# Low parts on GpSimd and a fourth seven-product unit in gate and up of a transformer block

## Chip, cores and metric

The kernel runs on one core of a Trainium2 chip. The metric is the device time of one execution in microseconds (us); before the change it is 1452.65 us (median of 3 runs, 1452.64 to 1453.78). Engines: TensorE (PE; PEld are its weight loads), VectorE (DVE), ScalarE (ACT), GpSimd (POOL) and SyncE (SP), which issues most of the transfers.

## What is computed

One block of an encoder on a sequence of 256 positions and width 2048: four mixers and an output product, cross attention with 256 memory positions, and a gated feed-forward layer with 5632 hidden units, everything in float32. The part that matters here is the last:

```python
D_FF = ((8 * D_MODEL // 3 + 255) // 256) * 256     # 5632

def swiglu(h, w_gate_up, w_down):
    gate, up = jnp.split(h @ w_gate_up, 2, axis=-1)
    return (jax.nn.silu(gate) * up) @ w_down
...
        x = x + swiglu(rms_norm(x, norm_g[l, 2]), w_gate_up[l], w_down[l])
    return rms_norm(x, final_norm_g)
```

## The kernel before, in words

**Splitting.** Products run at float32 accuracy on TensorE by splitting each operand into a high part, rounded to the type that TensorE multiplies (`F32R`), and a low part, the rest. One product of a 128 x 128 block of activations with 128 x 512 weights is then three matmuls: high by high, high by low, low by high (`Block.part`, lines 493 to 498). The weights come from memory as plain float32. `Stream.split` (line 150) makes the parts: ScalarE copies `raw` to `wh` with rounding (L156), and VectorE subtracts `wl = raw - wh` (L157).

**Stream.** All weights are laid out on the host in the order of their use, in slabs of 128 x 2048 (1 MB, one transfer by SyncE's queue, L136). `Stream.make` splits a slab in parts of 1024 columns, each into one buffer pair `wh`, `wl`; in gate and up there are five such pairs, and four slots for raw slabs. A part is made as soon as a pair is free, up to a bound, so some parts are ready ahead of TensorE.

**Gate and up.** `gate_up` goes over 11 columns `j` of 512 hidden units. For each it multiplies by 512 columns of gate and 512 of up, over 16 blocks of the inner dimension, taken in 8 pairs `i`. A plain pair is one slab: 2 inner blocks x 2 (gate, up) x 2 halves of the rows, 8 products of three matmuls, 24 in all. Its slab is two parts of 1024, hence two casts and two subtractions.

**Seven-product units.** For the pairs named by `sevens(j)` the 2 x 2 x 2 products are formed with seven products instead of eight, by sums of blocks (Winograd's form of Strassen's scheme): 21 matmuls. The sums of activation blocks are made once, ahead, by `left` (they stay in SBUF as `sh` and `sl`); the sums of weight blocks are made on VectorE in place in the raw slab (L189), and the slab is split in four parts of 512, 1024, 1024 and 1024. Before the change the units are pairs 1, 3 and 5 in every column, except the first, which has only 5. Four of the seven products go to banks of their own (`p1`, `p5`, `p7`, `p6`), which `combine` adds on VectorE after the last unit of the column (the copy of `p1` on ScalarE is L1000); three go to the banks of the plain pairs. `finish` then adds the two kinds of banks, applies silu and the product, transposes the hidden block on VectorE (`store_turned`, L525) and has GpSimd issue eight transfers to the `hidden` tensor in memory (L530). `finish` of one column runs during the first pairs of the next one.

**Other work of GpSimd's queue there.** `turn` writes the residual to `xrows`, transposed (L1077), and reads it back (L1081); `fetch` reads the stored hidden blocks for the down product (L941). All of these are transfers that wait for VectorE or for earlier transfers, and an engine's queue is served in order.

**Order.** Matmuls are in the order of the program. Side work is held in generators (`Background`), which are polled between products and step on by an estimate of time. The order of each engine's instructions is then settled by the framework when the program is built; `keep` ties the parts of a unit to their places, plain parts are not tied.

Of the kernel before, what the change touches and what calls it, by code (L numbers as in the profile page):

```python
# [13 lines left out]
F32 = mybir.dt.float32  # L14
# [4 lines left out]
ALU = mybir.AluOpType  # L19
# [31 lines left out]
GU = 16 * (40 + 16 + 16 + 32 + 16)  # L51

def sevens(j):

    return (1, 3, 5) if j else (5,)


FORMED = 6
# [20 lines left out]
DOWN = GU // 16 + 16 * DFF // 1024  # L79
# [6 lines left out]
def seven(slab):  # L86

    j, i = divmod(slab - GU // 16, 8)
    return slab in UNITS if slab >= DOWN else j >= 0 and i in sevens(j)
# [22 lines left out]
class Stream:  # L112
# [34 lines left out]
                return pool  # L147
        return None

    def split(self, pool, at, r, edges):  # L150

        nc = self.nc
        wh, wl = (pool.tile([P, 1088], F32R, name=t, tag=t) for t in ("wh", "wl"))
        wh, wl = wh[:, at:at + 1024], wl[:, at:at + 1024]
        for a, b in zip(edges, edges[1:]):
            nc.scalar.copy(wh[:, a:b], r[:, a:b])  # L156
            nc.vector.tensor_tensor(out=wl[:, a:b], in0=r[:, a:b], in1=wh[:, a:b].bitcast(F32), op=ALU.subtract)  # L157
        self.bg.dve(edges[-1], len(edges) - 1)
        self.items.append((pool, wh, wl))

    def make(self):

        nc, (slab, part) = self.nc, self.todo
        n = 16 * slab + 8 * part
        if n >= NBLK - HELD:
            parts = [(self.places.pop(0)) for _ in range(2)]
            r = self.raw(slab)[:, part * 1024:part * 1024 + 1024]
            for a, (wh, wl) in zip((0, 512), parts):
                nc.scalar.copy(wh, r[:, a:a + 512])
                nc.vector.tensor_tensor(out=wl, in0=r[:, a:a + 512], in1=wh.bitcast(F32), op=ALU.subtract)  # L170
            self.bg.dve(1024, 2)
            self.items.append((None, parts))
            self.todo = (slab + part, 1 - part)
            return True
        pool = self.free(slab)
        if pool is None:
            return False
        raw = self.raw(slab)
        at = 48 if any(a <= n < b for a, b in ROWS) else 8
        r = raw[:, part % 2 * 1024:part % 2 * 1024 + 1024]  # L180
        if not seven(slab):
            mark = len(nc.cur_bb.bb.instructions)
            self.split(pool, at, r, [0, 256, 512, 1024] if n == 0 else [0, 512, 1024] if n == 8 else [0, 1024])
            if DOWN <= slab < DOWN + 2 * AHEAD:
                self.keep(mark)
            self.todo = (slab + part, 1 - part)
            return True
        mark = len(nc.cur_bb.bb.instructions)
        op = lambda out, a, b, what=ALU.subtract: nc.vector.tensor_tensor(out=out, in0=a, in1=b, op=what)  # L189
        self.split(pool, at, r, [0, 512] if part == 0 else [0, 1024])  # L190
        b11, b12, b22, b21 = (raw[:, a:a + 512] for a in range(0, 2048, 512))
        if part == 0:
            blk = raw.rearrange("p (b c) -> p b c", b=4)
            op(r.rearrange("p (b c) -> p b c", b=2), blk[:, 0:3:2, :], blk[:, 1:2, :].to_broadcast([P, 2, 512]))
            self.bg.dve(1024)
        elif part == 1:
            op(b22, b22, b11, ALU.add)
            op(b21, b21, b22)
            self.bg.dve(1024, 2)
        self.keep(mark)  # L200
        self.todo = (slab + part // 3, (part + 1) % 4)
        return True
# [87 lines left out]
class Block:  # L290
# [665 lines left out]
    def gate_up(self, sw, gp, f):  # L956

        nc, st = self.nc, self.st
# [6 lines left out]

        def left():

            for i in (5, 1, 3):
                t = [self.tmp() for _ in range(2)]
                for x, k in zip(t, (2 * i, 2 * i + 1)):  # L970
                    nc.scalar.activation(x, self.resk(k), AF.Copy, scale=self.gvec(V_NG + 32, k))
                (a11, a21), (a12, a22) = ((x[:, 0:P], x[:, P:R]) for x in t)
                s = gp.tile([P, 512], F32, name="u", tag="u", bufs=2)
                s1, s2, s3, s4 = (s[:, a:a + P] for a in range(0, 512, P))
                self.stt(s1, a21, -1.0, a22, ALU.mult, ALU.subtract)
                self.stt(s2, s1, -1.0, a11, ALU.mult, ALU.subtract)
                self.tt(s3, a11, a21, ALU.subtract)
                self.tt(s4, a12, s2, ALU.subtract)
                yield
                h, l = sums[i] = [sw.tile([P, 512], F32R, name=f"s{x}{i}") for x in "hl"]  # L980
                self.split2(h, l, s)
                yield
# [44 lines left out]

        ready = [self.late, self.bg.add(norm())]
        forms = self.bg.add(left())
        turned = self.bg.add(self.turn())  # L1030
        early = end = None
        for j in range(DFF // 512):
# [5 lines left out]
            for i in range(8):  # L1038
                if j >= NUDGE and i in (2, 4, 7):
                    self.bg.nudge(turned if i == 2 else early)  # L1040
                if j == 0 and i == 6:
                    for g in ready:
                        self.bg.drain(g)
                if i == 1 and end:
                    self.bg.drain(end)
                if i in sevens(j):
                    if i == sevens(j)[0]:
                        if j == 0:
                            self.bg.drain(forms)
                        ps = [banks[1 - j % 2]() for _ in range(4)]  # L1050
                    unit(i, cs, ps, i == sevens(j)[0], i == sevens(j)[-1], *cols)
                    if i == sevens(j)[-1]:
                        s = [[gp.tile([P, 512], F32, name=f"{n}{r}", tag=f"{n}{r}") for n in "gh"] for r in range(2)]
                        last = combine(ps, s)
                        self.bg.add(last)
                    continue
                for k in (2 * i, 2 * i + 1):
                    for c in range(2):
                        wh, wl = st.take("w_gate_up", k, cols[c], 4)
                        for r in range(2):  # L1060
                            self.part_rows(cs[r][c], r, self.h3[k], wh, wl, k == 0, k == KT - 1)
                            self.bg.poll()
# [816 lines left out]
```

## Time and profile before

| | |
|---|---|
| median of 3 runs | 1452.65 us |
| the profiled execution | 1454.31 us, of it 1452.4 us from the first to the last instruction (its span) |
| mean granted TensorE clock | 0.998 |
| gate and up, from the first column's `combine` to the last one's (ten columns' time) | 414.8 us |

The page of the profile gives busy time by engine, the chain that ended last, and the costliest groups of instructions. A group's row has the line, the engine, the operation, what it writes and reads, the count, then busy time and mean duration in ns, then idle time in front of it and who ended it. A row of the timeline has its start, its length, engine and line, and in brackets the idle time before it; equal instructions that follow each other share a row (`x8`), and where shapes are mixed the row shows the first. A row of the stretches of time has the bounds, the busy time of each engine with the number of instructions, the granted clock, the share of transfers and their rate.

### The profile page before, as it was taken

What the parts mean: (1) busy time and instruction counts of PE and PEld (TensorE: products, weight loads), DVE (VectorE), ACT (ScalarE), POOL (GpSimd) and SP (SyncE); (2) the same over time, 40 slices, a digit from 0 to 9 for tenths busy, and PEclk for the clock granted to TensorE, in tenths of its full rate; (3) what the DMA queues carried; (4) which work ended last, traced back from release to release, by engine and by line L of the source; (5) the groups of instructions that cost most, each with busy time, mean ns of one, the idle gap of its engine ahead of it and who ended that gap; (6) DMA issues with size and microseconds to landing.
All of it is one profiled execution on the core that took longest, in us unless ns stands there. A gap on an engine that the chain in (4) does not pass through costs nothing.

```text
span 1452.4 us, 19765 instructions
## 1 busy us (share of the span) xinstructions
PE 1439.1 (99%) x7231; PEld 1217.8 (84%) x7231; DVE 1192.3 (82%) x1750; ACT 844.1 (58%) x1254; POOL 172.2 (12%) x294
## 2 busy tenths in 40 slices
PE   9999999999999999999999999999999999999997
PEld 8888888898899888888888888888888888788886
DVE  6587768778868767877778999999999997988875
ACT  6565655466656646765565555555655564655554
POOL 0220100000000001100003334112111112100000
PEclk9999999999999999999999999999999999999999
DMA  9985654454535656555555767666667656655654
GB/s 352 339 289 197 220 193 168 152 187 156 195 129 206 215 179 224 172 170 195 178 205 205 277 234 243 220 209 237 233 220 250 221 200 220 214 184 199 225 203 146
DMA packets 57394, 307.17 MB, mean 211 GB/s; under 512 B 9773, under 2 KB 11470, under 8 KB 25680
## 3 DMA queue, kind: packets, MB, share of 16 engines
q1 hardware_dynamic: 45920, 281.11, 54.9%
q0 software_dynamic: 10944, 24.14, 5.4%
q8 instruction: 57, 0.93, 0.3%
q10 hardware_dynamic: 432, 0.66, 0.1%
q14 instruction: 41, 0.34, 0.1%
HBM read 291.71 MB, written 14.16 MB: 211 GB/s over the span
## 4 chain that ended last, share of the span: by engine, by line
PE 94%; DVE 2%; issue 2%; ACT 1%; DMA 1%; POOL 1%; SPq 0%; DVEq 0%; POOLq 0%; ACTq 0%
PE pg L444 19%; PE pg L496 13%; PE pg L497 13%; PE pg L495 13%; PE pg L445 10%; PE pm L496 6%; PE pm L495 6%; PE pm L497 6%; PE pm L1380 1%; DVE wl L157 1%; PE pg L441 1%; PE pg L442 1%; PE pm L895 1%; PE pm L868 1%; DMA tmp<-hidden 1%
## 5 line engine op out<-in xcount | busy, mean ns | idle before, releaser
L156 ACT CAST wh<-raw 128x1024 fp32r<-128x1024 f32 (+1 forms) x589 | 589.2, 1013 | 466.6 <-PE pg L497 149.7
L157 DVE TENSOR_TENSOR wl<-raw,wh 128x1024 fp32r<-128x1024 f32 (+1 forms) x589 | 681.4, 1175 | 177.8 <-ACT wh L156 171.7
L444 PE MATMUL pg<-act,wh 128*128 128x512 f32 x1104 | 387.5, 393 | 0.0
L445 PE MATMUL pg<-act,wl 128*128 128x256 f32 x1216 | 340.7, 280 | 0.0
L496 PE MATMUL pg<-wl,act 128*128 128x512 f32 (+1 forms) x689 | 268.3, 389 | 1.5 <-DVE wl L157 1.4
L495 PE MATMUL pg<-wh,act 128*128 128x512 f32 (+1 forms) x689 | 268.7, 391 | 0.0
L497 PE MATMUL pg<-wh,act 128*128 128x512 f32 (+1 forms) x689 | 268.3, 389 | 0.0
L444 PEld LDWEIGHTS pg<-act,wh 128*128 128x128 f32 x1104 | 207.4, 188 | 44.9
L445 PEld LDWEIGHTS pg<-act,wl 128*128 128x128 f32 x1216 | 228.5, 188 | 0.8 <-DVE wl L157 0.5
L496 PEld LDWEIGHTS pg<-wl,act 128*128 128x128 f32 x689 | 129.5, 188 | 29.6 <-DVE wl L157 3.1
L495 PEld LDWEIGHTS pg<-wh,act 128*128 128x128 f32 x689 | 129.6, 188 | 27.5 <-issue 0.8
L497 PEld LDWEIGHTS pg<-wh,act 128*128 128x128 f32 x689 | 129.4, 188 | 27.4 <-issue 0.4
L496 PE MATMUL pm<-wl,act 128*128 128x512 f32 x318 | 123.7, 389 | 0.0
L497 PE MATMUL pm<-wh,act 128*128 128x512 f32 x318 | 123.7, 389 | 0.0
L495 PE MATMUL pm<-wh,act 128*128 128x512 f32 x318 | 123.6, 389 | 0.0
L189 DVE TENSOR_TENSOR raw<-raw 128x1024 f32<-128x1024 f32 x129 | 111.7, 866 | 3.0
L530 POOL DMA_DIRECT2D hidden<-u x88 | 56.8, 653 | 162.3 <-DVE u L525 139.7
L495 PEld LDWEIGHTS pm<-wh,act 128*128 128x128 f32 x318 | 59.7, 188 | 12.5
L497 PEld LDWEIGHTS pm<-wh,act 128*128 128x128 f32 x318 | 59.7, 188 | 12.4
L496 PEld LDWEIGHTS pm<-wl,act 128*128 128x128 f32 x318 | 59.7, 188 | 12.4
L1077 POOL DMA_DIRECT2D xrows<-tmp x64 | 37.0, 586 | 182.7 <-DVE rc L323 126.6
L941 POOL DMA_DIRECT2D tmp<-hidden x44 | 24.5, 560 | 145.7 <-DVE f L319 73.4
(361 smaller groups left out, 1778.6 us busy)
## 6 DMA issues: line engine op xcount, KB each, us to landing
raw<-in_W SPq DMA_DIRECT2D x246, 1024.0 KB, 5.0
raw<-in_W SPq DMA_DIRECT2D x11, 512.0 KB, 7.5
hidden<-u POOLq DMA_DIRECT2D x88, 64.0 KB, 4.4
tmp<-hidden POOLq DMA_DIRECT2D x44, 128.0 KB, 4.6
res<-in_xT SPq DMA_DIRECT2D x8, 512.0 KB, 8.4
k<-in_mem SPq DMA_DIRECT2D x8, 256.0 KB, 6.8
k<-in_x SPq DMA_DIRECT2D x8, 256.0 KB, 9.9
keys<-k POOLq DMA_DIRECT2D x32, 64.0 KB, 5.4
```

The lines of the kernel that those rows point to most:

```text
L156: nc.scalar.copy(wh[:, a:b], r[:, a:b])
L157: nc.vector.tensor_tensor(out=wl[:, a:b], in0=r[:, a:b], in1=wh[:, a:b].bitcast(F32), op=ALU.subtract)
L189: op = lambda out, a, b, what=ALU.subtract: nc.vector.tensor_tensor(out=out, in0=a, in1=b, op=what)
L441: self.nc.tensor.matmul(p[:, 0:R], wh, slot[:, 0:R], start=start, stop=False)
L444: self.nc.tensor.matmul(p[:, :], wh, slot[:, :], start=start, stop=False)
L445: self.nc.tensor.matmul(p[:, 0:R], wl, slot[:, 0:R], start=False, stop=stop)
L495: self.nc.tensor.matmul(p, hi, wh, start=start, stop=False)
L496: self.nc.tensor.matmul(p, hi, wl, start=False, stop=False)
L497: self.nc.tensor.matmul(p, lo, wh, start=False, stop=stop)
L530: nc.gpsimd.dma_start(to[:, :, 32 * a:32 * a + 32], u[32 * a:32 * a + 32, :].rearrange("f (b t) -> f b t", t=32))
L941: self.nc.gpsimd.dma_start(m[k], self.ff[k * P:(k + 1) * P, :])
L1077: nc.gpsimd.dma_start(to[:, :, c:c + 32], u[32 * a:32 * a + 32, :].rearrange("t (b f) -> t b f", f=32))
```

## The change

Pair 6 becomes a seven-product unit in all columns but the first, and `left` forms its sums too. In the same columns, the second part of each slab that stays plain (pairs 0, 2, 4 and 7) has its low part subtracted by GpSimd; it is not counted in the estimate of VectorE's work.

```diff
 def sevens(j):
 
-    return (1, 3, 5) if j else (5,)
+    return (1, 3, 5, 6) if j else (5,)
...
-    def split(self, pool, at, r, edges):
+    def split(self, pool, at, r, edges, other=False):
...
         for a, b in zip(edges, edges[1:]):
             nc.scalar.copy(wh[:, a:b], r[:, a:b])
-            nc.vector.tensor_tensor(out=wl[:, a:b], in0=r[:, a:b], in1=wh[:, a:b].bitcast(F32), op=ALU.subtract)
-        self.bg.dve(edges[-1], len(edges) - 1)
+            (nc.gpsimd if other else nc.vector).tensor_tensor(out=wl[:, a:b], in0=r[:, a:b], in1=wh[:, a:b].bitcast(F32), op=ALU.subtract)
+        if not other:
+            self.bg.dve(edges[-1], len(edges) - 1)
         self.items.append((pool, wh, wl))
...
         if not seven(slab):
             mark = len(nc.cur_bb.bb.instructions)
-            self.split(pool, at, r, [0, 256, 512, 1024] if n == 0 else [0, 512, 1024] if n == 8 else [0, 1024])
+            self.split(pool, at, r, [0, 256, 512, 1024] if n == 0 else [0, 512, 1024] if n == 8 else [0, 1024],
+                       part == 1 and GU // 16 + 8 <= slab < DOWN)
...
         def left():
 
-            for i in (5, 1, 3):
+            for i in (5, 1, 3, 6):
```

## Prediction

> **What bounds the kernel now.** I read the engine shares first, then the chain that ended last, then the busy times of the stage that the change touches: gate and up, between the first and the last partial-sum copy of `combine`, ten columns of 512 hidden units.
>
> ```profile
> span 1452.4 us, 19765 instructions
> PE 1439.1 (99%) x7231; PEld 1217.8 (84%) x7231; DVE 1192.3 (82%) x1750; ACT 844.1 (58%) x1254; POOL 172.2 (12%) x294
> PE 94%; DVE 2%; issue 2%; ACT 1%; DMA 1%; POOL 1%; SPq 0%; DVEq 0%; POOLq 0%; ACTq 0%
> ```
> ```profile
> core 0: us, PE busy (x) PEld busy (x) DVE busy (x) ACT busy (x) POOL busy (x), PEclk, DMA share, GB/s
> 779.50:1194.30 414.80, 414.80 (x1832) 343.47 (x1831) 394.99 (x455) 235.82 (x266) 91.71 (x150) 1.00 0.66 231
> 738.00:779.50 41.50, 41.50 (x202) 34.92 (x202) 34.21 (x67) 25.28 (x37) 14.98 (x26) 1.00 0.61 201
> ```
>
> TensorE is busy for all 414.80 us of ten columns, at granted clock 1.00: 41.48 us each. VectorE is busy for 394.99, 95%. So TensorE sets the pace and VectorE has 1.98 us a column to spare. What follows hangs on that margin.
>
> ```profile
> 964.39 0.39 PE L495 MATMUL pg<-wh,act 128*128 128x512 f32 x1
> ...
> 965.07 0.39 PE L495 MATMUL pm<-wh,sh 128*128 128x512 f32 x1
> 965.29 0.39 PE L496 MATMUL pm<-wl,sh 128*128 128x512 f32 x1
> 965.52 0.39 PE L497 MATMUL pm<-wh,sl 128*128 128x512 f32 x1
> 965.75 0.39 PE L495 MATMUL pm<-wh,act 128*128 128x512 f32 x1
> ```
>
> Matmuls show 0.39 us but start every 0.227 (965.07 to 965.75 is three). A column has three units of 21 and five plain slabs of 24: 183 x 0.227 = 41.5, the measured period, so there are no gaps. The first matmul on a formed sum (`sh`, 965.07) is the fourth of the unit at inner pair 1, so that unit begins at 964.39 and its column 24 x 0.227 = 5.44 earlier, at 958.95. Times "into the column" below count from there.
>
> **The change part by part.** *TensorE.* Pair 6 of ten columns becomes a unit: 3 matmuls fewer, 10 x 3 x 0.227 = **-6.8 us**. This is on the path, and it is the whole gain.
>
> *VectorE's own work.*
>
> ```profile
> 949.89 1.22 DVE L157 TENSOR_TENSOR wl<-raw,wh 128x1024 fp32r<-128x1024 f32 x1
> 951.02 0.68 DVE L319 TENSOR_TENSOR h<-pm,m 128x512 f32<-128x512 f32 x1
> 951.62 0.68 DVE L319 TENSOR_TENSOR g<-pm,m 128x512 f32<-128x512 f32 x1
> 952.22 1.22 DVE L157 TENSOR_TENSOR wl<-raw,wh 128x1024 fp32r<-128x1024 f32 x1
> 953.36 0.68 DVE L319 TENSOR_TENSOR h<-pm,g 128x512 f32<-128x512 f32 x1
> ...
> 957.11 0.69 DVE L319 TENSOR_TENSOR g<-pg,g 128x512 f32<-128x512 f32 x1 [0.80 <-PE pg L497]
> ...
> 965.46 1.30 DVE L525 STREAM_TRANSPOSE u<-h 128x512 f32<-128x512 f32 x2
> 966.68 2.92 DVE L157 TENSOR_TENSOR wl<-raw,wh 128x1024 fp32r<-128x1024 f32 x3
> ```
>
> From start to start, 512 elements take 0.60 and 1024 take 1.13 to 1.14; I use 1.13. Plain subtractions fall from ten to four a column (-6 x 1.13), and a unit adds 4 pieces of 1024 and 3 of 512 (4 x 1.13 + 3 x 0.60 = 6.32): net -0.46 a column, so VectorE would be busy 394.99 - 4.6 = 390.4 in ten columns. The sums for pair 6 in `left` are four small operations and one of 512, at most 5 x 0.60 = 3 us, in the first column, where VectorE is idle 41.50 - 34.21 = 7.3: nothing. Without that idle time it would be 3 us.
>
> *GpSimd's subtraction.* No row shows one. The nearest:
>
> ```profile
> L1580 POOL MEMSET gs<- 128x512 f32 x2 | 1.0, 526 | 123.8 <-DVE res L319 123.8
> masks.py:199 POOL TENSOR_SCALAR_AFFINE_SELECT ident<-ident 128x128 f32<-128x128 f32 x1 | 0.3, 287 | 0.1
> masks.py:197 POOL MEMSET ident<- 128x128 f32 x1 | 0.2, 204 | 0.3 <-POOLq L1858 0.3
> ```
>
> Writing costs (526 - 204) / 384 = 0.84 ns an element and 0.10 us fixed; a read adds (287 - 204) / 128 = 0.65 ns. Writes alone bound 1024 elements at 0.96 us from below, three passes at 0.84 at 2.68 from above. I take one write and two reads, 2.14 ns: **2.29 us**, because the select shows reads that are not hidden behind writes. Four a column, 91.6 us in all. GpSimd has the time (91.71 busy of 414.80).
>
> *Where it waits.* GpSimd's queue is served in order, and it issues the transfers of the hidden state.
>
> ```profile
> 966.46 5.14 POOL L530 DMA_DIRECT2D hidden<-u  x8 [31.26 <-DVE u L525]
> POOL tmp L941 <- DMA hidden<-u: 22.9, 4, 7.1
> 953.71 0.62 ACT L156 CAST wh<-raw 128x512 fp32r<-128x512 f32 x1 [1.67 <-PE pg L497]
> ```
>
> In the changed program's GpSimd queue the subtraction for pair 2 stands behind all eight issues of `hidden` in seven of ten columns (the first, second, fourth, fifth, seventh, ninth and tenth of those with units at 1, 3, 5, 6), and before them in three. Those issues wait for the transposes of `finish`. Before, the transposes start at 965.46, 6.51 into the column. With the last unit one pair later, `combine`'s four operations (2.4 us) fall into VectorE's run ahead of them; it had waits of about 1.1 there (0.80 in the row of 957.11 and 0.32 at the cast before it), so I take 1.3 later, 7.8. The first issue comes 1.0 after (966.46 - 965.46), the eight take 5.14, then the subtraction: 7.8 + 1.0 + 5.14 + 2.29 = 16.2. TensorE wants that low part at pair 2's second half: 5.44 + 4.76 + 2.72, and one matmul on, 13.15. It stands still 3.1. In the first of these columns `combine` is still early, so 1.8. Six x 3.1 + 1.8 = **+20.4 us**. With 0.96 or 2.68 for the subtraction this is 11 or 23. The cast of 953.71 starts 0.2 after the pair 6 that frees its buffer (953.51), five parts ahead: that is all the stock there is, and a part that is late by more than its lead stops TensorE. The fetches behind those issues (up to 7.1 us of waiting) can hold pair 4's subtraction in the first column; I leave that to the range.
>
> *Side by side or in turn.* Both engines now fetch two SBUF tensors per instruction. If GpSimd's subtraction holds VectorE up, VectorE loses between 0 and 2.29 us each time. The rows in which VectorE keeps its pace beside GpSimd (966.68 beside 966.46) are transfer issues, which fetch no tensor for arithmetic, so they do not speak for 0; the select's row, where GpSimd's own accesses add up, is the nearest to streams that take turns. I take the upper end. What does not fetch two SBUF tensors can still run beside it:
>
> ```profile
> L525 DVE STREAM_TRANSPOSE u<-h 128x512 f32<-128x512 f32 x20 | 13.0, 686 | 0.0
> L319 DVE TENSOR_TENSOR g<-pm,g 128x512 f32<-128x512 f32 x10 | 6.9, 687 | 3.4 <-PE pm L497 3.4
> L1074 DVE STREAM_TRANSPOSE tmp<-res 128x256 f32<-128x256 f32 x10 | 4.4, 436 | 0.0
> L319 DVE TENSOR_TENSOR g<-pg,m 128x512 f32<-128x512 f32 x5 | 3.4, 679 | 0.0
> ```
>
> Four groups like the second (10 each) and eight like the last (5 each) read PSUM: 4 x 6.9 + 8 x 3.4 + 13.0 + 4.4 = 72 of 395, 18%. So VectorE needs 390.4 + 0.82 x 91.6 = 465.5 for ten columns against 414.8: **+50.7**. Counted along the chain instead: the subtractions of pairs 7 and 0 hold VectorE just ahead of unit 1, 2 x 2.29, of which I let some 1.6 fall into its waits for buffers (an estimate), so it is 3.0 later and the seven columns stall 3.0 more. In the other three VectorE itself is late: pair 2's first low part, ready 967.81 - 958.95 = 8.86 into the column, comes 4.3 later against 10.43 wanted: 2.7. That gives 20.4 + 21.0 + 8.1 - 6.8 = **+42.7**. Between the two I take +47.
>
> The Trainium skill has a rule on this, on its page "SBUF — State Buffer", section "Who interferes with whom": a VectorE instruction with two SBUF inputs contends with a GpSimd instruction that reads SBUF. No run here shows it yet. By that rule the sum is the +47; with engines that do not meet it would be 20.4 - 6.8 = +13.6.
>
> *Hidden.* ScalarE gains 1.7 us of casts a column (1.05 and 0.62 a piece) at 236 of 415 busy: nothing; were it full, 17. Weight loads now wait for GpSimd too before a slot is overwritten, but the four slots are some 15 us of work ahead of transfers of 5.0:
>
> ```profile
> raw<-in_W SPq DMA_DIRECT2D x246, 1024.0 KB, 5.0
> ```
>
> Sum: span 1452.4 + 47 = 1499.4. The profiled execution took 1454.31, 1.9 more than its span; the median of the runs is 1452.65, 1.7 below it. On the median: **1499.5 us**.
>
> **Rivals.** *Queue only* (engines run side by side; low parts are late behind the `hidden` issues): 1452.65 + 13.6 = 1466, from 1457 to 1472 by the subtraction's bounds. For it: no row of VectorE slowed by GpSimd. Against: no row that tests it. *Gain*: the subtractions arrive in time, 1452.65 - 6.8 = 1446. Its place is pair 2's second half; it needs the eight issues to start before 13.15 - 2.29 - 5.14 = 5.7 into the column, where they now start at 7.5; with an average lateness under 6.8 / 7 = 0.97 us it still wins. For it: VectorE's work does not grow and TensorE's chain has no gap. Against: even with `combine` where it was, 7.5 + 5.14 + 2.29 = 14.9. *Worse*: the subtraction takes 2.68 or more and everything is in turn: 390.4 + 107 - 414.8 = +83, 1535. *Cancelled*: lateness eats just the gain, 1450 to 1455.5.
>
> **How the numbers follow.** In turn 0.50 (1482 to 1515), queue only 0.24, gain 0.14, worse 0.06, cancelled 0.06. A change under 0.2% (2.9 us) can't be told from none here. Faster 0.14, same 0.06, slower 0.80. The range takes in queue only and most of what is above the forecast: 1457 to 1522; gain, cancelled and the worst stay out.
>
> **What would show it.** In the new profile: 40 GpSimd subtractions near 2.3 us; 90 matmuls fewer, still 0.227 apart where they run; in gate and up, TensorE idle just before matmuls on `wl`, released by GpSimd at pair 2, with `hidden` issues right ahead of the subtraction. In turn: VectorE subtractions beside GpSimd's lengthened towards 2 to 3.4 us, its busy time near 100%, ten columns about 460. Queue only: VectorE's 1.22 unchanged, and stalls only at pair 2. The forecast is wrong if VectorE's durations beside GpSimd stay as they are, and its sign is wrong if no TensorE gap is released by GpSimd.

## The result, and the profile after

The changed kernel takes 1551.2 us (median of 4 runs, 1549.98 to 1554.23) against 1452.94 us of the kernel before beside it: a ratio of 1.0678, 95% interval 1.066 to 1.0697. That is 98.3 us slower, where 47 were forecast. The profiled execution has a span of 1548.2 us, 95.8 more than before. First its page, then the stretch from the first to the last `combine` copy:

```profile
span 1548.2 us, 19834 instructions
PE 1471.1 (95%) x7201; PEld 1225.0 (79%) x7201; DVE 1273.2 (82%) x1765; ACT 857.6 (55%) x1277; POOL 279.5 (18%) x334
```
```profile
core 0: us, PE busy (x) PEld busy (x) DVE busy (x) ACT busy (x) POOL busy (x), PEclk, DMA share, GB/s
779.60:1292.90 513.30, 449.72 (x1820) 354.23 (x1818) 471.85 (x461) 246.92 (x285) 195.15 (x187) 0.94 0.55 187
```

The stretch has grown from 414.80 to 513.30 us; the part before it takes 779.6 us as before (779.5), and the part after it is 2.8 us shorter, with some 20 matmuls fewer in it. TensorE, busy without a gap before, now is busy for 449.72 of 513.30, at a granted clock of 0.94 instead of 1.00. VectorE's busy time has grown by 77 us, although its own work was to fall, and yet it is idle for 41 us, where it was 20 before. (The stretch ends at a `combine` that now comes one pair later, so it holds some 20 matmuls beyond the ten columns' 1800, about 5 us.)

Where VectorE's time went shows in the groups of instructions of the whole changed kernel:

```profile
L157 POOL TENSOR_TENSOR wl<-raw,wh 128x1024 fp32r<-128x1024 f32 x40 | 108.5, 2723 | 140.0 <-ACT wh L156 123.8 <-issue 16.1
L157 DVE TENSOR_TENSOR wl<-raw,wh 128x512 fp32r<-128x512 f32 x56 | 50.8, 908 | 8.8 <-ACT wh L156 8.6
L191 DVE TENSOR_TENSOR raw<-raw 128x512 f32<-128x512 f32 x106 | 94.4, 890 | 2.4
```

VectorE instructions of 512 elements that took 686 ns on average now take about 900. Single ones, in the timeline, say why:

```profile
1022.04 2.46 POOL L157 TENSOR_TENSOR wl<-raw,wh 128x1024 fp32r<-128x1024 f32 x1 [5.54 <-issue]
1022.58 2.47 DVE L157 TENSOR_TENSOR wl<-raw,wh 128x512 fp32r<-128x512 f32 x1 [0.36 <-ACT wh L156]
...
1025.09 1.23 DVE L191 TENSOR_TENSOR raw<-raw 128x1024 f32<-128x1024 f32 x1
```

GpSimd subtracts from 1022.04 to 1024.50. VectorE starts a subtraction of 512 in the middle, at 1022.58, and ends it at 1025.05, 0.55 after GpSimd is through: it did nothing until then, and afterwards took its usual time. The same shows all over gate and up: each of the 36 VectorE instructions that took more than 1.3 us ended 0.28, 0.55 or 1.08 us (for 256, 512 or 1024 elements, give or take 0.01) after the end of a GpSimd subtraction. The two engines do take turns, by whole instructions.

A worse place, at pair 3 of a column, with all engines:

```profile
854.60 6.70 DVE L191 TENSOR_TENSOR raw<-raw 128x512 f32<-128x512 f32 x2
855.37 0.61 PE L497 MATMUL pm<-wh,sh 128*128 128x512 f32 x2
855.37 4.65 POOL L157 TENSOR_TENSOR wl<-raw,wh 128x1024 fp32r<-128x1024 f32 x2
...
861.34 1.04 ACT L156 CAST wh<-raw 128x1024 fp32r<-128x1024 f32 x1 [4.68 <-DVE raw L191]
862.44 0.80 PE L497 MATMUL pm<-wh,sh 128*128 128x512 f32 x1 [6.46 <-ACT wh L156]
863.03 0.63 PE L498 MATMUL pm<-wl,sh 128*128 128x512 f32 x1
863.46 0.63 PE L499 MATMUL pm<-wh,sl 128*128 128x512 f32 x1
```

Two GpSimd subtractions, both late behind the `hidden` issues, run back to back. Two VectorE sums that take 1.41 us elsewhere take 6.70: VectorE got no turn between the two. (The first sum had started 0.77 before GpSimd's recorded start and should have been done by then; the runs do not show why it was held all the same.) ScalarE's cast needs that sum, waits 4.68, and TensorE waits 6.46 for the cast. After the gap matmuls start 0.43 us apart instead of 0.227.

How the engines wait for each other in the stretch (us in total, times, longest us), before:

```profile
ACT wh L156 <- DVE raw L189: 69.6, 39, 2.7
ACT wh L156 <- PE pm L497: 50.4, 43, 2.1
ACT wh L156 <- PE pg L497: 49.8, 41, 2.1
DVE wl L157 <- ACT wh L156: 11.2, 15, 1.5
```

and after:

```profile
ACT wh L156 <- DVE raw L191: 130.1, 55, 5.4
ACT wh L156 <- PE pm L499: 59.3, 34, 4.4
ACT wh L156 <- PE pg L499: 55.9, 34, 7.4
DVE wl L157 <- ACT wh L156: 34.9, 24, 7.0
```

### The profile page after: what moved, and what is told of

It is laid out like the page before. It is cut to its first block, busy times and chain, and to the rows that moved or that the text cites. A ratio compares the mean times of both kernels' runs of the same rounds, so it can differ in the third digit from the quotient of the medians.

```text
span 1548.2 us, 19834 instructions
## 1 busy us (share of the span) xinstructions
PE 1471.1 (95%) x7201; PEld 1225.0 (79%) x7201; DVE 1273.2 (82%) x1765; ACT 857.6 (55%) x1277; POOL 279.5 (18%) x334
## 5 line engine op out<-in xcount | busy, mean ns | idle before, releaser
L156 ACT CAST wh<-raw 128x1024 fp32r<-128x1024 f32 (+1 forms) x609 | 601.9, 1006 | 545.2 <-PE pg L499 149.6
L157 DVE TENSOR_TENSOR wl<-raw,wh 128x1024 fp32r<-128x1024 f32 (+2 forms) x569 | 707.1, 1258 | 198.2 <-ACT wh L156 192.2
L498 PE MATMUL pg<-wl,act 128*128 128x512 f32 (+1 forms) x664 | 263.2, 396 | 7.9 <-DVE wl L157 4.3
L497 PE MATMUL pg<-wh,act 128*128 128x512 f32 (+1 forms) x664 | 257.6, 395 | 9.4 <-DVE g L321 5.6
L499 PE MATMUL pg<-wh,act 128*128 128x512 f32 (+1 forms) x664 | 262.5, 396 | 0.0
L191 DVE TENSOR_TENSOR raw<-raw 128x1024 f32<-128x1024 f32 x159 | 158.9, 1000 | 3.6
L497 PEld LDWEIGHTS pg<-wh,act 128*128 128x128 f32 x664 | 125.8, 189 | 40.4 <-DVE g L321 7.3
L499 PEld LDWEIGHTS pg<-wh,act 128*128 128x128 f32 x664 | 127.5, 192 | 27.4 <-issue 0.4
L157 POOL TENSOR_TENSOR wl<-raw,wh 128x1024 fp32r<-128x1024 f32 x40 | 108.5, 2723 | 140.0 <-ACT wh L156 123.8
L498 PE MATMUL pm<-wl,act 128*128 128x512 f32 x293 | 119.7, 409 | 5.9 <-POOL wl L157 4.0
L497 PE MATMUL pm<-wh,act 128*128 128x512 f32 x293 | 114.1, 404 | 9.3 <-DVE g L321 7.7
L499 PE MATMUL pm<-wh,act 128*128 128x512 f32 x293 | 118.8, 405 | 0.0
L497 PEld LDWEIGHTS pm<-wh,act 128*128 128x128 f32 x293 | 56.6, 193 | 26.4 <-DVE g L321 9.4
L499 PEld LDWEIGHTS pm<-wh,act 128*128 128x128 f32 x293 | 58.0, 198 | 12.6
```

The source lines that it names most:

```text
L157: (nc.gpsimd if other else nc.vector).tensor_tensor(out=wl[:, a:b], in0=r[:, a:b], in1=wh[:, a:b].bitcast(F32), op=ALU.subtract)
L497: self.nc.tensor.matmul(p, hi, wh, start=start, stop=False)
L498: self.nc.tensor.matmul(p, hi, wl, start=False, stop=False)
L499: self.nc.tensor.matmul(p, lo, wh, start=False, stop=stop)
```

## Experiments

Three readings were put against each other: A, the engines take turns at SBUF reads; B, no interference, only low parts that are late behind the `hidden` issues in GpSimd's queue; C and D, the fourth unit itself overloads VectorE, or leaves it late. Single runs are beside runs of the kernel before on the same chip (1453 to 1455 us).

**e1: the offload without the fourth unit.**

```diff
-    return (1, 3, 5, 6) if j else (5,)
+    return (1, 3, 5) if j else (5,)
...
-                       part == 1 and GU // 16 + 8 <= slab < DOWN)
+                       part == 1 and GU // 16 + 8 <= slab < DOWN and (slab - GU // 16) % 8 != 6)
```


> Units at pairs 1, 3 and 5 as before; GpSimd subtracts the second halves of the plain pairs 0, 2, 4 and 7 (40 subtractions, pair 6 stays on VectorE). Theory A (the two engines take turns at SBUF reads: a VectorE instruction with two SBUF inputs waits until GpSimd's subtraction is over): VectorE loses 4.5 us of own work a column and gains up to 9.6 us of waiting, so it is slower than before without any fourth unit: 1480 to 1535 us, with VectorE instructions lengthened by up to 2.4 us and TensorE gaps. Theory B (no interference, only low parts late behind the hidden issues): 1460 to 1475 us, VectorE durations unchanged, gaps only at pair 2. Theory C (the fourth unit itself overloads VectorE): within 3 us of 1453.

Measured 1489.8 us, in A's range. Relieving VectorE of forty subtractions costs 36 us by itself. In its stretch VectorE's busy time, fourth number, is above the 394.99 of before, although it has 45 us less to do (40 x 1.13):

```profile
779.60:1231.90 452.30, 429.29 (x1836) 349.01 (x1835) 414.92 (x419) 235.46 (x270) 190.90 (x192) 0.98 0.63 213
```

**e2: the fourth unit without the offload.**

```diff
-                       part == 1 and GU // 16 + 8 <= slab < DOWN)
+                       False)
```


> The fourth unit with all subtractions on VectorE. VectorE's own work becomes 39.5 + 6.3 - 2.3 = 43.5 us a column against 40.8 of TensorE, so VectorE sets the pace. Theory A: 1465 to 1490 us, clearly faster than the 1551 of the changed kernel, with no VectorE instruction lengthened. Theory B: the same 1465 to 1490. Theory C: near 1551.

Measured 1478.3 us. VectorE is the bound, busy for 98% of the stretch, and no instruction is lengthened:

```profile
779.40:1220.00 440.60, 423.47 (x1821) 337.85 (x1819) 431.92 (x501) 243.23 (x283) 92.60 (x152) 1.00 0.63 218
```

So each half of the change loses alone, and the offload makes the fourth unit 73 us worse instead of carrying it. C falls.

**e3: GpSimd writes but does not read.**

```diff
+            if other:
+                for w in (1024, 1024, 512):
+                    nc.gpsimd.memset(wl[:, 0:w].bitcast(F32), 0.0)
+            else:
+                nc.vector.tensor_tensor(...)
```


> As the changed kernel, but each GpSimd subtraction is replaced by three memsets of the same low part (1024, 1024 and 512 elements, about 2.45 us together by the memset row of before): GpSimd is as busy and its queue as long, but it reads nothing from SBUF. The low parts of these halves are left out of the products. Theory A: VectorE's 1024 subtraction is back at 1.22 us mean and its instructions are never held; what is left is lateness behind the hidden issues: 1446 to 1475 us. Theory A with writes counted too (any GpSimd access holds VectorE): still 1530 to 1560. Theory B: 1551, since the queue is unchanged. Theory C: 1551.

Measured 1481.5 us: 70 us come back by not reading. It is 6 us over the range that A had given, and 3.5 of them have nothing to do with the edit: TensorE lost them within the first 17 us of this execution, and the stretch begins at 783.10 instead of 779.60. In the stretch alone 71.5 us come back (513.30 to 441.80). The stretch, and the group of VectorE's subtractions:

```profile
783.10:1224.90 441.80, 424.23 (x1821) 340.72 (x1820) 392.47 (x463) 246.34 (x285) 183.22 (x266) 0.99 0.64 219
```
```profile
L162 DVE TENSOR_TENSOR wl<-raw,wh 128x1024 fp32r<-128x1024 f32 x511 | 617.6, 1220 | 189.7 <-ACT wh L156 177.4 <-issue 6.1 <-PE pg L452 2.1
```

They are back at 1220 ns, and VectorE is busy for 392.47, as its own work had been put (390.4). The 471.85 of the changed kernel thus hold 79.4 us in which VectorE is held, 2.04 for each of the 39 GpSimd subtractions that fall in the stretch. What remains of the loss needs no reading: the queue or the fourth unit.

**e4: SyncE issues the hidden transfers**, GpSimd still subtracts.

```diff
-            nc.gpsimd.dma_start(to[:, :, 32 * a:32 * a + 32],
+            (by or nc.gpsimd).dma_start(to[:, :, 32 * a:32 * a + 32],
...
-                self.store_turned(self.ff[j * 512:(j + 1) * 512, r * P:(r + 1) * P], u, h)
+                self.store_turned(self.ff[j * 512:(j + 1) * 512, r * P:(r + 1) * P], u, h, by=nc.sync)
```


> As the changed kernel, but SyncE issues the eight transfers of the hidden state, so no GpSimd subtraction stands behind them. Theory A: most of the loss stays, 1510 to 1550 us, with VectorE still lengthened. Theory B: the loss goes, 1446 to 1460 us. Theory C: 1551.

Measured 1531.8 us: clearing the queue gives 19 us back, 21 in the stretch, and the rest stays. B alone falls. VectorE is still held, busy for 462.57:

```profile
779.70:1272.00 492.30, 444.65 (x1820) 351.36 (x1818) 462.57 (x461) 245.58 (x285) 142.97 (x107) 0.95 0.59 195
```

**e5: both, memsets and SyncE.** The edits of e3 and e4 together.

> GpSimd writes three memsets instead of subtracting (these low parts are left out), and SyncE issues the hidden transfers: neither reads by GpSimd nor a queue in front of its work. Theory A with the queue as the rest (reading costs what e3 gave back, the order of GpSimd's queue the rest): 1446 to 1456 us, TensorE gaps under 10 us in all. Theory D (the fourth unit in a row after the third leaves VectorE late by itself, even when relieved of the subtractions): 1465 to 1482 us with gaps released by VectorE and ScalarE.

Measured 1454.3 us, against 1453.8 of before. TensorE is busy for 415.60 of its 416.80:

```profile
779.90:1196.70 416.80, 415.60 (x1820) 339.93 (x1819) 392.99 (x463) 246.76 (x284) 132.73 (x186) 1.00 0.69 232
```

Without reads and queue the loss is gone, but so is the gain of 6.8 us. The memsets wait for their buffer only and not for ScalarE's cast, so they come a little earlier than a subtraction could; the differences e3 and e5 are to be read with that.

**e6: the same subtractions in halves.**

```diff
+            for c, d in ((a, (a + b) // 2), ((a + b) // 2, b)) if other else ((a, b),):
+                (nc.gpsimd if other else nc.vector).tensor_tensor(out=wl[:, c:d], ...)
```


> The changed kernel with each GpSimd subtraction in two of 512 elements (80 of some 1.2 us). Theory A (an instruction holds the other engine for its whole length, and VectorE gets its turn between two): the total held time stays, but a VectorE instruction waits at most some 1.2 us at a time, so fewer gaps over 2.9 us: 1500 to 1545 us. If the hold were not by instruction but by accesses: 1545 to 1560 us.

Measured 1539.4 us, 12 less than the changed kernel, within A's range. VectorE is busy for 468.6 us, hardly less: the sum of the holds is the same. Most VectorE instructions that are held now take 2.35 us at most, but six took 3.9 to 6.3, through two or four halves in a row, so "at most some 1.2 us at a time" does not hold. Of the 12 us, some 7 are time of matmuls 0.43 us apart (65 of them, 13 us beyond 0.227 each, where the changed kernel has 101, 20 us).

**e7: one subtraction a column**, three units, pair 4 alone.

```diff
-    return (1, 3, 5, 6) if j else (5,)
+    return (1, 3, 5) if j else (5,)
...
-                       part == 1 and GU // 16 + 8 <= slab < DOWN)
+                       part == 1 and GU // 16 + 8 <= slab < DOWN and (slab - GU // 16) % 8 == 4)
```


> Units at 1, 3 and 5; GpSimd subtracts only the second half of pair 4, ten subtractions in all, clear of the hidden issues. Theory A: VectorE is relieved of 1.1 us a column and held for up to 2.4, within the 2 us that it has to spare: 1452 to 1459 us. Theory B: 1451 to 1454 us.

Ratio 1.0012, interval 1.0002 to 1.0022 (10 runs). TensorE has no gap; VectorE, freed of ten subtractions (11.3 us), is busy for 403.44 instead of 394.99:

```profile
779.80:1195.00 415.20, 415.20 (x1832) 343.75 (x1831) 403.44 (x448) 236.03 (x270) 118.64 (x163) 1.00 0.68 232
```
```profile
L157 DVE TENSOR_TENSOR wl<-raw,wh 128x512 fp32r<-128x512 f32 x30 | 39.7, 1323 | 3.3 <-ACT wh L156 3.1
```

(8.45 + 11.3) / 10 = 1.98 us held for each, close to the 2.04 of e3. Less the 1.13 that VectorE is relieved of, this is 0.85 us a column, and VectorE has 2 to spare: the time grows by some 1.5 us (1455.3 against 1453.77).

**e8 and e10: GpSimd reads one tensor instead of two**, by copying the raw half.

```diff
+            if other:
+                nc.gpsimd.tensor_copy(wl[:, a:b], r[:, a:b])
```


> Units at 1, 3 and 5 with ten GpSimd copies of the raw half of pair 4 (one SBUF input) in place of subtractions; the low parts are wrong by that and not used for accuracy. Theory A: a GpSimd instruction with one SBUF input holds VectorE's two-input instructions for its whole length too: VectorE rows beside it are lengthened by up to the copy's length; 1450 to 1456 us. Theory A for two inputs only: no VectorE row is lengthened.

The kernel that ran as e8 was not the one described: it kept the fourth unit and copied in all four plain pairs, forty copies. It took 1487.9 us with VectorE busy for 420.5, between e3 (392.5, no reads) and the changed kernel (471.9, two reads). e10 is the one described:

> Units at 1, 3 and 5; GpSimd copies the raw half of pair 4 (one SBUF input, some 1.05 us) instead of subtracting it with VectorE relieved of it, ten in all; these ten low parts are wrong by that. If a GpSimd instruction with one SBUF input holds VectorE's two-input instructions for its whole length: VectorE rows beside a copy lengthened by up to 1.05 us, VectorE's busy time about 395 - 11 + 8 = 392 us, time 1451 to 1455 us. If one input does not hold it: no row lengthened, 384 us busy, the same time.

Measured 1455.1 us, VectorE busy for 393.04, 9.3 more than its own 383.7 (394.99 - 11.3), close to the 392 for the case that one input holds it. The copies took 1.05 us where nothing was in their way (two of the ten) and 1484 ns on average:

```profile
779.30:1194.60 415.30, 415.09 (x1832) 343.38 (x1831) 393.04 (x448) 237.39 (x269) 108.18 (x163) 1.00 0.68 232
```
```profile
L158 POOL CAST wl<-raw 128x1024 fp32r<-128x1024 f32 x10 | 14.8, 1484 | 33.5 <-issue 17.0 <-PE pg L501 9.6 <-PE pm L501 7.0
```

**e9: the fourth unit in three columns, no offload**, an attempt at a faster kernel.

```diff
-    return (1, 3, 5) if j else (5,)
+    return (1, 3, 5, 6) if j in (2, 5, 8) else (1, 3, 5) if j else (5,)
```


> No GpSimd subtraction; the fourth unit only in columns 2, 5 and 8, so that VectorE's spare 2 us a column (19.8 in ten) can take the 3 x 4.1 us of extra work. If the spare time can be used across columns: 3 x 0.68 = 2.0 us less than before, 1450 to 1452 us. If VectorE's spare time can't be used where the units stand in a row: TensorE gaps in those three columns and 1453 to 1462 us.

Ratio 1.0024, interval 1.0014 to 1.0034 (9 runs): slower by 3.3 us. VectorE is busy for 405.87 of 419.30 in the stretch, so it had time on the whole; but TensorE waits for it, up to 1.8 us at a time:

```profile
PEld pm L496 <- DVE wl L157: 3.6, 4, 1.8
PEld pg L496 <- DVE wl L157: 2.4, 3, 1.8
```

The waits are not in columns 2, 5 and 8, which take 40.8 to 41.2 us for their 180 matmuls (40.8 without a gap), but in the column after each, which takes 42.8 to 43.7 instead of 41.5; TensorE loses most of it at pair 2. VectorE's spare time in the columns that follow comes too late for that place. No version beat the kernel before.

## Why the prediction was right or wrong

**TensorE, -6.8 us: right.** The profile has 30 matmuls fewer (7231 to 7201). The "90" among the signs to look for was a slip; the sum used 10 x 3. They run 0.227 apart wherever the clock is full.

**VectorE's own work, 390.4 us: right.** 392.5 and 393.0 without reads.

**GpSimd's 2.29 us: right.** 2.33 to 2.46 in the sixteen shortest of the forty; 2.72 on average, since VectorE holds GpSimd up too: nine of them took 3.18 to 3.43, about one VectorE subtraction longer.

**In turn, with 82% of each subtraction falling on VectorE: right.** 75 us were forecast, 79.4 measured, and VectorE's busy time was put at 465.5 and came to 471.9. The sign "its busy time near 100%" did not come: it was 92% of the stretch. The rule of the Trainium skill ("SBUF — State Buffer", "Who interferes with whom") holds in these runs: held with reads (2.47 for 0.68 us), not held by memsets (1220 ns).

**The queue, +20.4 us: right.** In the stretch it is 21.0 from e4 against the changed kernel and 25.0 from e5 against e3. The places fit too: in e3, with the queue and without reads, the seven columns that the prediction names lost 28 us of TensorE's time in all (0.9 to 7.4 each, where 1.8 and 3.1 were forecast), the other three 2. (The queue rival's upper bound, 1472, was a slip: 1452.65 - 6.8 + 23 is 1469.)

**How these were put together, "+47": wrong, and this is the step that failed.** The first count said "VectorE needs 390.4 + 0.82 x 91.6 = 465.5 for ten columns against 414.8: +50.7". It takes the time for VectorE's busy time, as though an engine that becomes the bound were never idle, so that its 24 us of spare time would take up the first part of the holds and the queue's delay would vanish behind them. Even the rival *worse*, which counts in the same way, is 16 us short with its 1535. In fact VectorE was idle for 41.5 us. It feeds TensorE through ScalarE, and ScalarE waits for its sums and for buffers that TensorE frees; each stop passes round this ring. The rows of waits above show it: ScalarE's casts waited 130 us for VectorE's sums and 115 for TensorE, and VectorE's subtractions 35 us for those casts, where it was 11 before.

The second count followed the chain, and its term for the holds was too small: 21.0 + 8.1 = 29 us, where the runs show 72 to 76. It put "3.0" on a column for the two subtractions ahead of unit 1, and nothing for the others. By the starts of its matmuls (what each took beyond 0.227 us after the one before, at full clock, put down to a pair by its place in the order) TensorE lost 39 us at pair 2 in the changed kernel, but also 23 at pair 0, 12 at pair 6 and 6.5 at pair 3; in e4, with holds and no queue, most was lost at pairs 6 and 7 (27 and 13). Rows such as 854.60 show one kind, at pair 3, where a late subtraction meets the next one and both hold VectorE in one go.

In the stretch, reading costs 71.5 us (changed kernel - e3) or 75.5 (e4 - e5), the queue 21.0 or 25.0. The two orders differ by 4, so the terms hardly overlap: they have to be added, where the first count let one vanish behind the other. With -6.8 for the unit and 7 that the fourth unit costs by itself (e5, 1454.3, against 1453.8 - 6.8) this makes 97 of the 98; that the sum comes out is no proof, since the terms are differences of the same runs. The price of reading is near the 79 us in which VectorE is held, but in part by chance: some 17 us of it are time of matmuls 0.43 us apart.

**The fourth unit in a row with the third: not priced.** I gave it no cost, since VectorE's sum over a column fell. e5 shows 7 us for ten columns and e9, with the gain, some 5 for three. Of the 7, the starts of the matmuls show 4 to 5 in gate and up, most of it at pairs 6 and 3; the rest lies outside, and a single execution does not settle it. A unit asks VectorE for 6.3 us in 4.76 of TensorE, so two in a row would outrun the five buffers; no run with more buffers tested this.

**TensorE's clock: not foreseen.** In the changed kernel about a hundred matmuls start 0.43 us apart, some 20 us beyond 0.227 each; in e4 it is 85 and 17 us, in e3 15 and 3, in e5 two. This lies inside the terms above, not beside them, and nearly all of it in the price of reading. How much of it delayed the end, rather than passing while VectorE was the later one, was not tried.

## What to carry to other kernels

Moving an elementwise operation with SBUF inputs from VectorE to GpSimd is no relief where VectorE's other work also reads two SBUF tensors: here a subtraction that VectorE does in 1.13 us held it for about 2. Price the hold first, and then add it to every other delay rather than let spare time absorb it, when the engines feed each other through few buffers. And an engine with spare time over a whole column may have none where the work comes in a bunch: look at the densest place and at what follows it, not at the mean.

## What was not expected of the hardware

Two GpSimd subtractions in a row held VectorE through both: 5.3 us for two sums (6.70 against 1.41), so a waiting VectorE instruction is not always served between them. In e6 one took 6.3 us, through four halves. A GpSimd copy with one SBUF input holds VectorE as well (e10: 9.3 us in ten copies), while three memsets do not.

After all ten TensorE gaps of 2.89 us or more in the changed kernel (from one matmul's start to the next, up to 6.84), matmuls of 512 columns started 0.43 us apart until 3 to 9 us after the gap before returning to 0.227, as after 862.44. Single gaps of 2.30 us or less were followed by none of it; two close together, 1.47 and 1.16 us, were, but two others, 1.31 and 1.08, were not. No length parts the two kinds: in e4 a gap of 3.20 us (to 937.21) was not followed by it, and one of 2.30 (to 1034.75) was. The Trainium skill ("TensorE: Matmul & The Clock Gate", "Part 1: The HAM clock gate") describes a half-rate clock after an idle window of some 3.4 us that runs free of the kernel; the gaps of 2.30 and of 2.89 to 3.04 us that were followed by half rate here are shorter, those of 3.5 to 6.84 us agree.
